# Sums left to accumulating transfers, and transposes taken two blocks at a time: one change to a two-layer trunk on one Trainium2 core

## The chip, the core and the metric

The kernel runs on one NeuronCore of one Trainium2 chip, as one launch. The metric is the device time of the program in microseconds. Before the change it is 2697.47 us, the median of three runs (2697.16 to 2699.16). The engines are called as in the profile: PE is TensorE, DVE is VectorE, ACT is ScalarE, POOL is GpSimd, SP is SyncE, which here only starts transfers; PEld are TensorE's loads of stationary operands.

## What is computed

Two layers over 2048 tokens of 1024 features. Layer 0 is a pooling mixer; it does not change here. Layer 1 projects to queries and a gate z, attends to one shared set of keys and values, multiplies by SiLU(z), projects back, adds the residual, and then adds a gated embedding. Cut to that layer:

```python
def stick_breaking_attention(q, k, v):          # (B, H, S, d), 16 heads of 64
    for blk in range(S // Q_BLOCK):
        logits = q_blk @ k.T * SB_SCALE
        mask = s_idx < t_idx                    # strictly causal
        log_keep = where(mask, log_sigmoid(-logits), 0)
        later = cumsum(log_keep, reverse=True) - log_keep
        a = where(mask, exp(log_sigmoid(logits) + later), 0)
        o = a @ v

x = x + (o * silu(z)) @ b_w_out                 # called x3 in the kernel
x = x + (p[1] @ ple_w[1]) * sigmoid(x @ ple_gate_w[1])
```

All matrices and activations are float32.

## The kernel before

Every activation is held transposed, features on the 128 partitions and tokens along the free axis, in four chunks of 512 tokens (`c` or `s` from 0 to 3). To keep float32 accuracy a matmul is done as three: each operand is split into a rounded half and the rest, both stored as a pair `[P, 2, 512]` (`pr[:, 0]` and `pr[:, 1]`), and high by high, high by low and low by high are summed (L994, L996, L998).

Up to about 1340 us the first layer and all projections run. The attention behind it is one loop over steps `n`. A slot is a query chunk, a head and a key chunk; each has four steps `j`. Query chunks run from 3 down to 0 and have 256, 192, 128 and 64 steps. The stages of one block are set off by numbers of steps:

- `front` (step 4i + j): two matmuls (L924, L925) make the logits of 128 queries by 512 keys in a `psl` buffer; ACT takes their sigmoid into one of four `kap` buffers (L928); `scan` multiplies the remaining stick along the keys on VectorE (L936, on the diagonal L933) into a `pp` tile of the pool `ppool`.
- `turn` (LAG_T = 6 steps behind): for 128 keys `kt`, four transposes on TensorE (L949; on the diagonal 4, 3, 2, 1) turn the `pp` tiles of a slot into a `psa` buffer, of which there are two. ACT copies it rounded into an `at` pair (L952), and VectorE subtracts for the rest (L953); then the buffer is free.
- `gather` (LAG_G = 8 steps behind): two matmuls (L961, L962) of values by the `at` pair add into `pso`. Behind the last one of a head, ACT copies (L976, L977), VectorE adds two halves (L979), ACT adds a bias (L972) and GpSimd multiplies by the gate (L974).

Between these, a generator called `filler` fills TensorE: so many matmuls per step, by the function `shares` for chunks 3 and 2 and by a mean (`even`) for 1 and 0. In chunk 3's stage the filler computes the gates (`gate_z`, with L1028 and L1033); for three of the chunks it takes a `psa` buffer out of turn (L1020), and `load_ends` does so for all four (L910). In the stages of chunks 2, 1 and 0 it is `post(3)`, `post(2)` and `post(1)`; `post(0)` runs alone at the end.

`post(c)` has two halves of eight outputs of 128 features each. In the first, the output projection is added to the residual on VectorE (`xr`, L1068), and `halves` splits the sum into the pair `x3[o]` (ACT L1072, GpSimd L1073). In the second, a gate (`sg`, ACT L1092) is multiplied by the embedding's product `pl` (L1106), and then x3 is added back from its two halves: the low one on GpSimd (L1107), the high one two steps later on VectorE (L1108). `finish` sends the result from SP (L1112), one output later. `xr`, `sg` and others share the tag `tmp` with four buffers.

The order on each engine is set by the program's order for instructions under `keep_in_program_order` (`stay`), and by a scheduler for the others. Every engine works through its own queue in order; SP's transfers wait in that queue too. Around the change stand these lines of the step loop:

```python
for n in range(4 * len(slots) + LAG_G):
    now[0] = n
    i2, j2 = divmod(n - LAG_T, 4)
    if 0 <= i2 < len(slots):
        turn(active[i2], j2)
```

Of the kernel before, what the change touches and what calls it, by code (L numbers as in the profile page):

```python
# [10 lines left out]
F32R = mybir.dt.float32r  # L11
AF = mybir.ActivationFunctionType
ALU = mybir.AluOpType
AX = mybir.AxisListType

P = 128
# [6 lines left out]
W5 = 512  # L23
# [7 lines left out]
def f(ap):  # L31
    return ap.bitcast(F32)
# [3 lines left out]
def trunk_kernel(ctx, tc, x, xt, pt0, wut, cols, heads, zin, grp, aout, agate, aple,  # L36
                 bq, kv, bz, bout, bgate, bple, outt):
    nc = tc.nc
    V, A, G, T = nc.vector, nc.scalar, nc.gpsimd, nc.tensor
# [179 lines left out]
    with ExitStack() as st:  # L219
# [3 lines left out]
        t2 = st.enter_context(tc.tile_pool(name="t2", bufs=2))  # L223
# [631 lines left out]

    with ExitStack() as st:
        kap = st.enter_context(tc.tile_pool(name="kap", bufs=1))
        ppool = st.enter_context(tc.tile_pool(name="ppool", bufs=12))
        t2 = st.enter_context(tc.tile_pool(name="s2", bufs=2))
        psa = st.enter_context(tc.tile_pool(name="psa", bufs=2, space=bass.MemoryType.PSUM))  # L860
        pso = st.enter_context(tc.tile_pool(name="pso", bufs=2, space=bass.MemoryType.PSUM))
# [13 lines left out]
        due, now, tail = [], [0], [0]  # L875

        def soon(k, fn):

            if tail[0]:
                fn()  # L880
                return lambda: None
            item = (now[0] + k, len(due), fn)
            due.append(item)

            def force():
                if item in due:
                    due.remove(item)
                    fn()

            return force  # L890
# [52 lines left out]
        def turn(st, kt):  # L943

            j0 = kt if st["diag"] else 0
            pt = psa.tile([P, W5], F32, tag="psa", name="psa")
            for j in range(j0, 4):
                pp, r0 = st["a"][j]
                T.transpose(pt[:, j * P : (j + 1) * P], pp[:, r0 + kt * P : r0 + (kt + 1) * P], ident)  # L949
            at = t2.tile([P, 2, W5], F32R, tag="at", name="at", bufs=3)  # L950
            cs = slice(j0 * P, W5)
            A.copy(out=at[:, 0, cs], in_=pt[:, cs])  # L952
            V.tensor_tensor(out=at[:, 1, cs], in0=pt[:, cs], in1=f(at[:, 0, cs]), op=ALU.subtract)  # L953
            st["at"][kt] = at
# [89 lines left out]
        def post(c):  # L1044

            pin = t2.tile([P, 2, W5], F32, tag="pin", name="pin", bufs=1)
            nc.sync.dma_start(out=pin, in_=pt0[1, :, c * W5 : (c + 1) * W5].rearrange("(k q) n -> q k n", q=P))
            x3, og, held = [], ogs[c], tc.keep_in_program_order
            while len(og) < 8:
                pair_up(c)  # L1050
            settle()
            both = []
            for o in range(KT):
                xr = t2.tile([P, W5], F32, tag="tmp", name="xr", bufs=4)
                if not c and o < 2:
                    if not o:
                        both = [(stored(wod[e]), dense()) for e in range(2)]
                        for e, (wo, ps) in enumerate(both):
                            yield from piecewise(ps, wo, og, 0, 0, KT - 1)
                    wo, ps = both[o]  # L1060
                    nc.sync.dma_start(out=xr, in_=x2d[c][o])
                    yield from piecewise(ps, wo, og, 0, KT - 1)
                else:
                    wo = stored(wod[o])
                    nc.sync.dma_start(out=xr, in_=x2d[c][o])
                    ps = dense()
                    yield from piecewise(ps, wo, og, 0)
                V.tensor_tensor(out=xr, in0=ps, in1=xr, op=ALU.add)  # L1068
                pr = pair("x3")

                def halves(pr=pr, xr=xr):
                    stay(A.copy(out=pr[:, 0], in_=xr))  # L1072
                    G.tensor_tensor(out=pr[:, 1], in0=xr, in1=f(pr[:, 0]), op=ALU.subtract)  # L1073

                made = soon(1, halves)
                x3.append(pr)
            pt_ = []
            for k in range(2):
                pr = t2.tile([P, 2, W5], F32R, tag="ple", name="ple")
                held(A.copy(out=pr[:, 0], in_=pin[:, k]))  # L1080
                held(V.tensor_tensor(out=pr[:, 1], in0=pin[:, k], in1=f(pr[:, 0]), op=ALU.subtract))
                pt_.append(pr)
            yield
            made()
            late = []
            for o in range(KT):
                wg = stored(wgd[o])
                wl = stored(wld[o])
                ps = dense()
                yield from piecewise(ps, wg, x3, 0)  # L1090
                sg = t2.tile([P, W5], F32, tag="tmp", name="sg", bufs=4)
                made = soon(1, lambda sg=sg, ps=ps: stay(A.activation(out=sg, in_=ps, func=AF.Sigmoid)))  # L1092
                pl = dense()
                yield from piecewise(pl, wl, pt_, 0)
                made()
                if tail[0] and o == KT - 1:
                    whole = t2.tile([P, W5], F32, tag="tmp", name="x3w", bufs=4)
                    V.tensor_tensor(out=whole, in0=f(x3[o][:, 0]), in1=f(x3[o][:, 1]), op=ALU.add)
                    for cs in (slice(0, 256), slice(256, W5)):
                        V.tensor_tensor(out=sg[:, cs], in0=pl[:, cs], in1=sg[:, cs], op=ALU.mult)  # L1100
                        V.tensor_tensor(out=sg[:, cs], in0=sg[:, cs], in1=whole[:, cs], op=ALU.add)
                        if late:
                            late.pop()()
                        nc.sync.dma_start(out=outt[o * P : (o + 1) * P, c * W5 + cs.start : c * W5 + cs.stop], in_=sg[:, cs])
                    continue
                V.tensor_tensor(out=sg, in0=pl, in1=sg, op=ALU.mult)  # L1106
                (V if tail[0] else G).tensor_tensor(out=sg, in0=sg, in1=f(x3[o][:, 1]), op=ALU.add)  # L1107
                summed = soon(2, lambda o=o, sg=sg: V.tensor_tensor(out=sg, in0=sg, in1=f(x3[o][:, 0]), op=ALU.add))  # L1108

                def finish(o=o, sg=sg, summed=summed):  # L1110
                    summed()
                    nc.sync.dma_start(out=outt[o * P : (o + 1) * P, c * W5 : (c + 1) * W5], in_=sg)  # L1112

                if late:
                    late.pop()()
                late.append(finish)
                if c:
                    pair_up(c - 1)
                yield
            if late:  # L1120
                late.pop()()
            yield
# [38 lines left out]
        slots = []  # L1161
# [4 lines left out]
        active, filler, owed, head = {}, beside(NSUB - 1), 0.0, {}  # L1166
        LAG_T, LAG_G = 6, 8
# [19 lines left out]

        for n in range(4 * len(slots) + LAG_G):
            now[0] = n
            i2, j2 = divmod(n - LAG_T, 4)  # L1190
            if 0 <= i2 < len(slots):
                turn(active[i2], j2)
            i, j = divmod(n, 4)
            scan = None
            if i < len(slots):
                c, h, kc = slots[i]
# [91 lines left out]
```

## Time and profile before

| | |
|---|---|
| time, median of three runs | 2697.47 us |
| the profiled execution's own time | 2696.51 us |
| its span, from first to last instruction | 2694.7 us |
| granted TensorE clock over the span | 1.00 |
| transposes L949 | 2176, mean 273 ns |
| L953, rest of the transposed block (VectorE) | 640, mean 596 ns |
| L936, full scan (VectorE) | 384, mean 1336 ns |
| L1107, low half of x3 (GpSimd) | 24, mean 1392 ns |
| L1108, high half of x3 (VectorE) | 31, mean 954 ns |
| VectorE's stand for L1107 before L1108 | 18.1 us in 12 waits |
| transfers' share of the 16 DMA engines, SP's queue | 64.5% |

The mean of a matmul is longer than the distance between two starts, since matmuls are pipelined; starts are what counts. In the rows of a group, the columns are the line, the engine, the operation, the tiles, the number of instructions, then busy time and mean, and the idle time ahead of them with the engine and line that ended it. In a timeline row the first two numbers are the start and the duration, and a bracket holds the idle time ahead of the instruction. A list of waits gives who waited for whom: total, times, and the longest.

### The profile page before, as it was taken

What the parts mean: (1) busy time and instruction counts of PE and PEld (TensorE: products, weight loads), DVE (VectorE), ACT (ScalarE), POOL (GpSimd) and SP (SyncE); (2) the same over time, 40 slices, a digit from 0 to 9 for tenths busy, and PEclk for the clock granted to TensorE, in tenths of its full rate; (3) what the DMA queues carried; (4) which work ended last, traced back from release to release, by engine and by line L of the source; (5) the groups of instructions that cost most, each with busy time, mean ns of one, the idle gap of its engine ahead of it and who ended that gap; (6) DMA issues with size and microseconds to landing.
All of it is one profiled execution on the core that took longest, in us unless ns stands there. A gap on an engine that the chain in (4) does not pass through costs nothing. (4 is left out here: it accounts for less than half of the span.)

```text
span 2694.7 us, 38618 instructions
## 1 busy us (share of the span) xinstructions
PE 2673.6 (99%) x13352; PEld 2226.5 (83%) x13352; DVE 1941.9 (72%) x2506; ACT 1399.0 (52%) x2735; POOL 922.0 (34%) x724
## 2 busy tenths in 40 slices
PE   9999999999999999999999999999999999999999
PEld 8888888888888888888878888888888888888887
DVE  6776626755367643755399999999999998986632
ACT  6445523555135541445366666666666666665531
POOL 2675338643485434753121111122111211222220
PEclk9999999999999999999999999999999999999999
DMA  8657785567856678444788665555655576668865
GB/s 328 222 168 279 252 302 193 198 229 254 300 180 223 242 241 305 145 150 149 223 239 281 195 210 173 163 165 181 198 164 173 173 214 199 197 198 262 268 226 172
DMA packets 276688, 581.56 MB, mean 216 GB/s; under 512 B 33126, under 2 KB 67174, under 8 KB 276492
## 3 DMA queue, kind: packets, MB, share of 16 engines
q1 hardware_dynamic: 270754, 571.41, 64.5%
q10 hardware_dynamic: 5738, 7.68, 1.0%
q8 instruction: 106, 1.74, 0.3%
q14 instruction: 90, 0.74, 0.1%
HBM read 438.40 MB, written 132.19 MB: 212 GB/s over the span
## 5 line engine op out<-in xcount | busy, mean ns | idle before, releaser
L952 ACT CAST at<-psa 128x512 fp32r<-128x512 f32 (+3 forms) x640 | 334.3, 522 | 439.1 <-PE psa L949 429.4
L614 PE MATMUL psd<-wpair,x 128*128 128x512 f32 x2304 | 536.8, 391 | 0.0
L936 DVE TENSOR_TENSOR_SCAN pp<-kap,pp,zeros 128x512 f32<-128x512 f32 x384 | 513.1, 1336 | 6.1 <-ACT kap L928 5.1
L614 PEld LDWEIGHTS psd<-wpair,x 128*128 128x128 f32 x2304 | 429.8, 188 | 87.1
L953 DVE TENSOR_TENSOR at<-psa,at 128x512 fp32r<-128x512 f32 (+3 forms) x640 | 381.3, 596 | 82.0 <-ACT at L952 77.3
L949 PE MATMUL psa<-ident,pp 128*128 128x128 f32 x2176 | 344.6, 273 | 10.7 <-DVE at L953 10.3
L928 ACT ACTIVATE kap<-psl 128x512 f32<-128x512 f32 (+3 forms) x640 | 345.0, 539 | 13.2 <-PE psl L925 10.3
L949 PEld LDWEIGHTS psa<-ident,pp 128*128 128x128 f32 x2176 | 265.4, 140 | 77.7 <-DVE at L953 21.9
L924 PE MATMUL psl<-kk,qa 128*128 128x512 f32 (+3 forms) x640 | 282.3, 441 | 0.1
L962 PE MATMUL pso<-at,vv 128*128 128x512 f32 (+3 forms) x640 | 234.4, 366 | 1.3 <-DVE at L953 1.3
L925 PE MATMUL psl<-kk,qb 128*128 128x512 f32 (+3 forms) x640 | 232.9, 364 | 0.0
L961 PE MATMUL pso<-at,vv 128*128 128x512 f32 (+3 forms) x640 | 232.8, 364 | 0.1
L933 DVE TENSOR_TENSOR_SCAN pp<-kap,ahead 128x128 f32<-128x128 f32 (+3 forms) x256 | 227.0, 887 | 5.1 <-ACT kap L928 3.2
L167 PE MATMUL psd<-xp,wpair 128*128 128x512 f32 x512 | 199.5, 390 | 1.7 <-DVE xp L316 1.7
L166 PE MATMUL psd<-xp,wpair 128*128 128x512 f32 x512 | 200.0, 391 | 0.4 <-ACT xp L315 0.3
L168 PE MATMUL psd<-xp,wpair 128*128 128x512 f32 x512 | 199.3, 390 | 0.0
L149 DVE SCALAR_TENSOR_TENSOR wpair<-wraw,gains,wpair 128x512 fp32r<-128x512 f32 x192 | 161.4, 883 | 48.9 <-ACT wpair L148 48.9
L143 POOL TENSOR_TENSOR wpair<-wraw,wpair 128x512 fp32r<-128x512 f32 x99 | 144.0, 1464 | 84.2 <-ACT wpair L141 78.8
L148 ACT ACTIVATE wpair<-wraw,gains 128x512 fp32r<-128x512 f32 x192 | 132.7, 718 | 68.9 <-DMA wraw<-in_bq_dram 31.1
L1033 POOL TENSOR_TENSOR zr<-zr,sgz 128x512 f32<-128x512 f32 x32 | 62.0, 1938 | 307.1 <-ACT sgz L1032 269.2
L141 ACT CAST wpair<-wraw 128x512 fp32r<-128x512 f32 x148 | 89.9, 618 | 122.1 <-PE psd L168 98.9
L962 PEld LDWEIGHTS pso<-at,vv 128*128 128x128 f32 x640 | 120.3, 188 | 27.7 <-DVE at L953 1.7
(200 smaller groups left out, 5365.7 us busy)
## 6 DMA issues: line engine op xcount, KB each, us to landing
kk<-kd SPq DMA_DIRECT2D x320, 128.0 KB
vv<-vd SPq DMA_DIRECT2D x160, 256.0 KB
wraw<-in_kv_dram SPq DMA_DIRECT2D x128, 256.0 KB
wpair<-wzd SPq DMA_DIRECT2D x64, 512.0 KB
wpair<-wod SPq DMA_DIRECT2D x64, 512.0 KB
wpair<-wgd SPq DMA_DIRECT2D x64, 512.0 KB
wpair<-wu SPq DMA_DIRECT2D x48, 512.0 KB
wpair<-wi SPq DMA_DIRECT2D x36, 512.0 KB
```

Source lines behind the costliest of these rows:

```text
L166: T.matmul(ps, wst(units, kt, 0, c0), acts[kt][:, 0], start=(begin and kt == order[0]), stop=False)
L614: T.matmul(pss2[i], ck["x2"][kt][:, xh, tk], wst(ws, kt, wh, 0, W5), start=(kt == 0 and xh == 0 and wh == 0), stop=(kt == KT - 1 and wh == 1))
L924: T.matmul(ps[:, :w], qa[:, qs], kk[:, :w], start=True, stop=False)
L925: T.matmul(ps[:, :w], qb[:, qs], kk[:, :w], start=False, stop=True)
L928: A.activation(out=kp[:, r0:], in_=ps[:, :w], func=AF.Sigmoid, scale=-1.0)
L933: V.tensor_tensor_scan(out=pp[:, r0:][:, ::-1], data0=kp[:, r0:][:, ::-1], data1=ahead[:, r0:][:, ::-1], initial=1.0, op0=ALU.mult, op1=AL ...
L936: V.tensor_tensor_scan(out=pp[:, ::-1], data0=kp[:, ::-1], data1=zeros.to_broadcast([P, W5]), initial=st["carry"][j], op0=ALU.mult, op1=AL ...
L949: T.transpose(pt[:, j * P : (j + 1) * P], pp[:, r0 + kt * P : r0 + (kt + 1) * P], ident)
L952: A.copy(out=at[:, 0, cs], in_=pt[:, cs])
L953: V.tensor_tensor(out=at[:, 1, cs], in0=pt[:, cs], in1=f(at[:, 0, cs]), op=ALU.subtract)
L961: T.matmul(po[:, cs], vv[:, kt, :], at[:, 0, cs], start=(st["diag"] and kt == 0), stop=False)
L962: T.matmul(po[:, cs], vv[:, kt, :], at[:, 1, cs], start=False, stop=(st["last"] and kt == 3))
```

## The change

There are two parts, and two pools change size with the second.

The first part concerns the query chunks 3 and 2 (`c > 1`). As soon as `xr` is summed, SP writes it to the output (L1072 of the changed kernel). The two adds of x3 are left out; `finish` sends the gated embedding `sg` from GpSimd's queue as a transfer that adds to what lies in the output (L1119). Chunks 1 and 0 stay as they were.

The second part concerns `turn`: in even steps it is called for two blocks, the one that is due and the next, and in odd steps not at all. Every second block is turned one step earlier. `at` has four buffers where it had three, and `ppool` ten where it had twelve.

```diff
-        ppool = st.enter_context(tc.tile_pool(name="ppool", bufs=12))
+        ppool = st.enter_context(tc.tile_pool(name="ppool", bufs=10))
...
-            at = t2.tile([P, 2, W5], F32R, tag="at", name="at", bufs=3)
+            at = t2.tile([P, 2, W5], F32R, tag="at", name="at", bufs=4)
...
                 V.tensor_tensor(out=xr, in0=ps, in1=xr, op=ALU.add)
                 pr = pair("x3")
+
+                if c > 1:
+                    nc.sync.dma_start(out=outt[o * P : (o + 1) * P, c * W5 : (c + 1) * W5], in_=xr)
...
                 V.tensor_tensor(out=sg, in0=pl, in1=sg, op=ALU.mult)
-                (V if tail[0] else G).tensor_tensor(out=sg, in0=sg, in1=f(x3[o][:, 1]), op=ALU.add)
-                summed = soon(2, lambda o=o, sg=sg: V.tensor_tensor(out=sg, in0=sg, in1=f(x3[o][:, 0]), op=ALU.add))
-
-                def finish(o=o, sg=sg, summed=summed):
+                whole = outt[o * P : (o + 1) * P, c * W5 : (c + 1) * W5]
+                summed = lambda: None
+                if c < 2:
+                    (V if tail[0] else G).tensor_tensor(out=sg, in0=sg, in1=f(x3[o][:, 1]), op=ALU.add)
+                    summed = soon(2, lambda o=o, sg=sg: V.tensor_tensor(out=sg, in0=sg, in1=f(x3[o][:, 0]), op=ALU.add))
+
+                def finish(sg=sg, summed=summed, whole=whole):
                     summed()
-                    nc.sync.dma_start(out=outt[o * P : (o + 1) * P, c * W5 : (c + 1) * W5], in_=sg)
+                    if c > 1:
+                        nc.gpsimd.dma_start(out=whole, in_=sg, accum_op=ALU.add)
+                    else:
+                        nc.sync.dma_start(out=whole, in_=sg)
...
             now[0] = n
-            i2, j2 = divmod(n - LAG_T, 4)
-            if 0 <= i2 < len(slots):
-                turn(active[i2], j2)
+            for m in (n, n + 1) if n % 2 == 0 else ():
+                i2, j2 = divmod(m - LAG_T, 4)
+                if 0 <= i2 < len(slots):
+                    turn(active[i2], j2)
```

What this does to the order of the engines is shown at three places, all in the stage of query chunk 2, where the second half of `post(3)` begins.

TensorE, two steps before the change: in each step the transposes, the logits, some matmuls of the filler, and the gather.

```order
L949 MATMUL psa<-ident,pp 128x128 x4
L924 MATMUL psl<-kk,qa 128x512
L925 MATMUL psl<-kk,qb 128x512
L996 MATMUL psd<-og,wpair 128x512
L998 MATMUL psd<-og,wpair 128x512
L961 MATMUL pso<-at,vv 128x512
L962 MATMUL pso<-at,vv 128x512
L949 MATMUL psa<-ident,pp 128x128 x4
L924 MATMUL psl<-kk,qa 128x512
```

The same two steps of the changed kernel:

```order
L949 MATMUL psa<-ident,pp 128x128 x8
L924 MATMUL psl<-kk,qa 128x512
L925 MATMUL psl<-kk,qb 128x512
L996 MATMUL psd<-og,wpair 128x512
L998 MATMUL psd<-og,wpair 128x512
L961 MATMUL pso<-at,vv 128x512
L962 MATMUL pso<-at,vv 128x512
L924 MATMUL psl<-kk,qa 128x512
```

Eight transposes stand where four stood, and the second step begins with its logits. On the diagonal the runs are of seven and three.

VectorE at the first two outputs of that half, before the change (`x_19137` is the pair x3 of the first output; the scan has the operation's name SCALAR_TENSOR_TENSOR here):

```order
L936 SCALAR_TENSOR_TENSOR pp<-kap_12442,pp,zeros 128x512
L1106 TENSOR_TENSOR sg<-psd,sg 128x512
L953 TENSOR_TENSOR at<-psa,at 128x512
L936 SCALAR_TENSOR_TENSOR pp<-kap_12443,pp,zeros 128x512
L1108 TENSOR_TENSOR sg<-sg,x_19137 128x512
L953 TENSOR_TENSOR at<-psa,at 128x512
L936 SCALAR_TENSOR_TENSOR pp<-kap_12444,pp,zeros 128x512
L953 TENSOR_TENSOR at<-psa,at 128x384
L936 SCALAR_TENSOR_TENSOR pp<-kap_12445,pp,zeros 128x512
```

And of the changed kernel, where L1109 is the product that was L1106:

```order
L953 TENSOR_TENSOR at<-psa,at 128x512 x2
L936 SCALAR_TENSOR_TENSOR pp<-kap_12442,pp,zeros 128x512
L1109 TENSOR_TENSOR sg<-psd,sg 128x512
L936 SCALAR_TENSOR_TENSOR pp<-kap_12443,pp,zeros 128x512
L953 TENSOR_TENSOR at<-psa,at 128x512
L953 TENSOR_TENSOR at<-psa,at 128x384
L936 SCALAR_TENSOR_TENSOR pp<-kap_12444,pp,zeros 128x512
L936 SCALAR_TENSOR_TENSOR pp<-kap_12445,pp,zeros 128x512
```

The L953 stand in twos ahead of two scans, and the add L1108 is gone.

SP's queue of the changed kernel around the first of the new writes (`wod`, the weights of the output projection; `qd`, `kd`, `vd`, the stored queries, keys and values):

```order
L212 DMA wpair<-wod_275 128x1024
L1072 DMA out_dram<-xr 128x512
L192 DMA qa<-qd_2_210 64x512 x2
L193 DMA qb<-qd_2_210 64x512 x2
L1065 DMA xr<-x2d_4_132 128x512
L212 DMA wpair<-wod_276 128x1024
L200 DMA kk<-kd_2_242 64x512 x2
```

The row L1072 is new; the loads behind it wait with it.

## The prediction, as it was put on record

> **What bounds the kernel now.** I read the page's busy table first, then the same table by stage of the attention, then the list of waits, and last the timeline around single waits.
>
> ```profile
> span 2694.7 us, 38618 instructions
> PE 2673.6 (99%) x13352; PEld 2226.5 (83%) x13352; DVE 1941.9 (72%) x2506; ACT 1399.0 (52%) x2735; POOL 922.0 (34%) x724
> ```
>
> TensorE is busy for 99% of the span. The change removes no matmul, so it can win only what TensorE idles (21 us in all) or a cost between its instructions. It touches the attention alone, which I cut into stages by query chunk (three rows: chunk 3, chunk 2, chunk 1; columns: length, busy time of PE, PEld, DVE, ACT, POOL, clock, DMA share, GB/s):
>
> ```profile
> 1361.00:1889.00 528.00, 524.34 (x2897) 436.81 (x2898) 514.06 (x614) 342.77 (x687) 89.82 (x49) 1.00 0.65 201
> 1889.00:2200.00 311.00, 306.91 (x1704) 256.83 (x1703) 302.25 (x370) 203.60 (x422) 53.70 (x32) 1.00 0.57 180
> 2200.00:2440.00 240.00, 236.76 (x1310) 199.42 (x1309) 213.04 (x278) 153.04 (x336) 46.12 (x31) 1.00 0.69 204
> ```
>
> VectorE is nearly as full as TensorE in chunks 3 and 2 (514 of 528 and 302 of 311 us). Who keeps TensorE waiting stands in the list of waits, taken for the same three stretches (the first from 1340) and for the end of the attention:
>
> ```profile
> PE psa L949 <- DVE at L953: 3.0, 6, 1.2
> PE psae L910 <- DVE at L953: 0.6, 1, 0.6
> ...
> PE psa L949 <- DVE at L953: 4.1, 5, 1.0
> ...
> PE psa L949 <- DVE at L953: 3.2, 6, 1.1
> ...
> PE pso L962 <- DVE at L953: 1.3, 1, 1.3
> ```
>
> It is always one wait: the transposes (L949) write a psa buffer that VectorE (L953) has not emptied yet. There are 3.0, 4.1 and 3.2 us of it in chunks 3, 2 and 1. How one arises, in chunk 1:
>
> ```profile
> 2333.47 1.29 POOL L1107 TENSOR_TENSOR sg<-sg,x 128x512 f32<-128x512 f32 x1 [13.12 <-PE psl L925]
> ...
> 2334.79 1.76 DVE L1108 TENSOR_TENSOR sg<-sg,x 128x512 f32<-128x512 f32 x1 [0.99 <-POOL sg L1107]
> ...
> 2336.47 1.27 DVE L936 TENSOR_TENSOR_SCAN pp<-kap,pp,zeros 128x512 f32<-128x512 f32 x1
> ...
> 2336.68 0.34 PE L962 MATMUL pso<-at,vv 128*128 128x384 f32 x1
> 2337.67 0.39 DVE L953 TENSOR_TENSOR at<-psa,at 128x256 fp32r<-128x256 f32 x1
> ...
> 2338.11 0.66 PE L949 MATMUL psa<-ident,pp 128*128 128x128 f32 x4 [1.10 <-DVE at L953]
> ```
>
> VectorE stands 0.99 us for GpSimd's add, adds for 1.76, then owes a scan and the L953 that TensorE needs. TensorE idles 1.10.
>
> **First part of the change: the sums of chunks 3 and 2 leave VectorE and GpSimd.** In chunk 2 (first row) and chunk 1 (second row) the final add costs VectorE
>
> ```profile
> L1108 DVE TENSOR_TENSOR sg<-sg,x 128x512 f32<-128x512 f32 x8 | 9.6, 1195 | 0.8 <-POOL sg L1107 0.8
> ...
> L1108 DVE TENSOR_TENSOR sg<-sg,x 128x512 f32<-128x512 f32 x7 | 9.0, 1284 | 5.6 <-POOL sg L1107 5.6
> ```
>
> so 9.6 + 0.8 us in chunk 2 and 9.0 + 5.6 in chunk 1 disappear from it (the eighth of the second set falls just behind 2440). That alone is worth nothing; it counts where a TensorE wait follows. Four of the five waits of chunk 2 and five of the six of chunk 1 start within 3.5 us behind an L1108. The first and the last of these nine pairs, and the one wait of chunk 1 that is no pair:
>
> ```profile
> 2063.09 1.70 DVE L1108 TENSOR_TENSOR sg<-sg,x 128x512 f32<-128x512 f32 x1
> ...
> 2065.45 0.55 PE L949 MATMUL psa<-ident,pp 128*128 128x128 f32 x3 [0.30 <-DVE at L953]
> ...
> 2407.43 1.77 DVE L1108 TENSOR_TENSOR sg<-sg,x 128x512 f32<-128x512 f32 x1 [1.12 <-POOL sg L1107]
> ...
> 2409.85 0.66 PE L949 MATMUL psa<-ident,pp 128*128 128x128 f32 x4 [0.63 <-DVE at L953]
> ...
> 2439.24 0.63 PE L949 MATMUL psa<-ident,pp 128*128 128x128 f32 x4 [0.27 <-DVE at L953]
> ```
>
> Each of the nine is shorter (at most 1.10) than the VectorE time that goes ahead of it (the add with its stand), so I let all nine go. They hold 4.1 - 1.04 = 3.0 us of idle time in chunk 2 and 3.2 - 0.27 = 3.0 in chunk 1. The one that stays in chunk 2 (1.04) has another cause, a GpSimd product beside a scan:
>
> ```profile
> 2050.63 1.27 DVE L936 TENSOR_TENSOR_SCAN pp<-kap,pp,zeros 128x512 f32<-128x512 f32 x1
> ...
> 2052.21 1.29 POOL L974 TENSOR_TENSOR os<-os,zt 128x512 f32<-128x512 f32 x1 [10.67 <-ACT os L972]
> 2052.41 2.17 DVE L936 TENSOR_TENSOR_SCAN pp<-kap,pp,zeros 128x512 f32<-128x512 f32 x1
> ...
> 2053.78 0.40 PE L962 MATMUL pso<-at,vv 128*128 128x512 f32 x1
> ...
> 2055.22 0.66 PE L949 MATMUL psa<-ident,pp 128*128 128x128 f32 x4 [1.04 <-DVE at L953]
> ```
>
> Beside GpSimd's product the scan takes 2.17 us instead of 1.27, so removing sixteen GpSimd adds also spares scans; I count that inside the nine waits. The same rows show what a wait costs: L949 starts 1.44 us after L962 where 0.23 is the rule, so 1.21 are lost where the view says 1.04. With 0.17 more for each of nine, the term is **-(3.0 + 3.0 + 1.5) = -7.5 us**; its bounds are 0 (VectorE owes the time elsewhere) and -9.2 (all eleven waits of chunks 2 and 1).
>
> What replaces the adds: sixteen more 256 KB writes on SP's queue (L1072) and sixteen accumulating transfers of 256 KB on GpSimd's queue in the place of L1107. The trace has no accumulating transfer. GpSimd is busy 54 of 311 and 46 of 240 us; if issuing one cost it as much as the add's 1.3 us, nothing on TensorE's path would notice, and if it cost nothing, neither. But if it slowed scans as the add does, part of the 7.5 would stay: between 0 and +4, and I take 0, since the row nearest to it is a transfer, not an add that reads two tiles. SP waits in order, and behind L1072, which waits for L1068, stand loads of qa, kk and vv. The waits of SP between 1889 and 2440:
>
> ```profile
> SPq L1112 <- DVE sg L1108: 32.1, 11, 5.1
> ...
> SPq L1065 <- POOL x L1073: 24.4, 8, 6.2
> ```
>
> SP already stood up to 5.1 us for L1108 in the same way, and 6.2 for an xr buffer, without any TensorE wait on a transfer in the list above. L1112 leaves SP for these chunks while L1072 comes: 0, with 0 to +3 as bounds. The transfers hold sg longer, but tmp has four buffers, so an sg comes back four outputs later, and chunk 2's stage makes sixteen outputs in 311 us, 19 us each: 78 us later, no wait.
>
> **Second part: two blocks' transposes together.** Is there a cost at the joint between transposes and matmuls? One transpose between full matmuls, then four:
>
> ```profile
> 1704.93 0.39 PE L962 MATMUL pso<-at,vv 128*128 128x512 f32 x1
> ...
> 1705.16 0.27 PE L949 MATMUL psa<-ident,pp 128*128 128x128 f32 x1
> ...
> 1705.50 0.39 PE L925 MATMUL psl<-kk,qb 128*128 128x512 f32 x1
> ...
> 1460.87 0.39 PE L962 MATMUL pso<-at,vv 128*128 128x512 f32 x1
> 1461.10 0.60 PE L949 MATMUL psa<-ident,pp 128*128 128x128 f32 x4
> ...
> 1461.77 0.39 PE L925 MATMUL psl<-kk,qb 128*128 128x512 f32 x1
> ```
>
> From L962 to L925 are 0.57 us with one and 0.90 with four: 0.11 for each transpose. Two full matmuls take 0.46, so 0.57 - 0.46 - 0.11 leaves nothing for the joint, within 0.01. 320 joints go: between -3 and +3 us, and I take **-1**, since the same difference over all undisturbed groups (31 with one, 189 with four) is 0.000 to 0.007.
>
> The Trainium skill ("TensorE: Matmul & The Clock Gate", Part 2, step 1) has a rule against this: weight loads are pulled ahead of running matmuls. By it the first load of each group hides behind L962, a merged pair hides one load instead of two, and with the page's 128/1.2 = 107 ns against 56 ns for the matmul 320 x 0.05 = 16 us are lost. The rows do not agree: one transpose costs the same 0.11 as each of four, since L924 behind it is late in turn (0.48 us long where L925 has 0.39).
>
> The price is the double buffer. Before, VectorE alternates L953 and scan; now it does two L953, then two scans. A pair's second group needs the second L953, which ends 0.68 behind the first (row below), while the first group gives 4 x 0.11 = 0.44: the margin shrinks by 0.25 at each pair. How often is it that thin? A transpose's weight load may start with the matmul ahead, 0.23 early, so its waits in chunk 3 count the thin places:
>
> ```profile
> PEld psa L949 <- DVE at L953: 9.1, 17, 1.6
> ...
> L953 DVE TENSOR_TENSOR at<-psa,at 128x512 fp32r<-128x512 f32 x123 | 83.0, 675 | 5.8 <-ACT at L952 4.5
> ```
>
> 17 of 256 steps. Those in the middle of a pair vanish as places, so I take ten: 10 x 0.25 = **+2.5**, bounds 0 and 128 pairs x 0.25 = +32. Of the 3.0 us in chunk 3 a part stands at odd steps, whose check goes, but most of that lateness reappears at the next pair: **-1**, a third, with -3 and 0 as bounds. Seven places take a psa buffer out of turn (L910, L1020); behind a pair that buffer was filled in the same step, but three matmuls now stand ahead of it: **+0.5**, bounds 0 and 7 x 0.6 = +4. The last block is turned one step earlier, which shortens the wait of 1.3 at the end: **-0.5**, bounds -1.3 and 0. ScalarE (343 of 528 us) and the smaller ppool (next use two steps behind the last reading) cost nothing.
>
> **Sum:** -7.5 - 1 + 2.5 - 1 + 0.5 - 0.5 = -7.0 us. The profiled execution took 2696.5 us (span 2694.7), 1.0 below the median of the three runs, 2697.5. Against the median the forecast is **2690.5 us**.
>
> **The rivals.** *The waits only move* (0.10): VectorE's bursts in chunks 2 and 1 also come from L1068, L979 and L1106, and pairs are checked more strictly, so half of the 7.5 is given back: 2694. For it speaks the wait at 2055, which has no L1108; against it that nine of eleven have one. *The transfers disturb as the adds did* (0.10): issuing them slows scans, or SP's loads come late: +4, 2694.5, or with SP's +3 about 2697. *Pairs starve TensorE* (0.12, the slower side): in chunk 3, where nothing is relieved and VectorE has 14 us of air in 528, the second group of a pair waits its 0.25 routinely. Ten pairs are in the sum; beyond the seven won and 5.4 more it needs 12.4/0.25, so 50 further pairs: from 60 of 128 on the kernel is slower, and with all it stands at 2720. For it speaks VectorE's 97%; against it that only 17 steps are thin now. *A merged pair loses half a transpose* (0.02), 0.055 at each of 320 pairs, since only one weight load of a run stands free: 17.6 us, 2709; the two groups measured above speak against it. (That is the Trainium skill's rule of the pull-ahead.) *Better than forecast* (0.06): all waits of chunks 3 to 1 go and pairs cost nothing: 2678 to 2684. That the scheduler undoes the pairs is excluded: the order of TensorE shows runs of seven and eight.
>
> **How the numbers follow.** The forecast has 0.60 with its own range of 2684 to 2695. A measurement can tell about 0.2% (5.4 us) from no change, so the lines are 2692.1 and 2702.9. Of the 0.60, 0.50 lie below; with 0.06, faster has 0.56. Same has 0.10 of the forecast and both middle rivals, 0.30. Slower has 0.14. The range 2682 to 2701 leaves out about 0.04 below and 0.14 above.
>
> **What would show it.** Right: waits of L949 for L953 in chunks 2 and 1 fall from 7.3 us to about 1.5, chunk 3 has 3 to 6, eight transposes take 0.88 us from first start to the next matmul, and no wait on a transfer appears. Wrong: chunk 3's waits above 12 us (pairs starve), scans of 2 us beside the GpSimd transfers, or TensorE waits named after kk, vv or wod.

## The result, and the profile after

The changed kernel takes **2689.52 us** (median of eight runs, 2688.59 to 2690.98) beside 2697.22 us for the kernel before on the same chip (eight runs, 2695.92 to 2699.16). The ratio is 0.9971, with a 95% interval of 0.9962 to 0.9981: 7.7 us faster. Two executions in the experiments, one of the kernel before (6391 us, beside runs 8 and 10 to 12) and one of run 11 (3630 us), were far slower than all others and are in no median below. The forecast was 2690.5 us, range 2682 to 2701. Lines of the changed kernel have new numbers: L1109 is the product that was L1106, L1072 the new write, L1119 the accumulating transfer.

The head of the page of the changed kernel, and its group of transposes (instructions, busy time and mean, idle time ahead of them):

```profile
span 2688.0 us, 39378 instructions
...
PE 2673.2 (99%) x13352; PEld 2237.9 (83%) x13352; DVE 1917.1 (71%) x2490; ACT 1391.2 (52%) x2735; POOL 904.0 (34%) x724
...
L949 PE MATMUL psa<-ident,pp 128*128 128x128 f32 x2176 | 295.6, 274 | 4.4 <-DVE at L953 3.9
```

TensorE does the same work (2673.2 us where it was 2673.6), and the span is 6.7 us shorter: nearly all that went is idle time. The same three stretches as in the prediction, and in them the waits of TensorE (the first two rows belong to 1340 to 1889, the third to 1889 to 2200; from 2200 to 2592 there is none):

```profile
1361.00:1889.00 528.00, 522.87 (x2882) 439.31 (x2881) 511.71 (x611) 338.86 (x683) 82.66 (x47) 1.00 0.64 200
1889.00:2200.00 311.00, 310.41 (x1729) 264.29 (x1727) 295.23 (x367) 205.21 (x428) 49.57 (x33) 1.00 0.63 191
2200.00:2440.00 240.00, 239.97 (x1335) 204.97 (x1333) 208.63 (x275) 152.57 (x339) 42.70 (x32) 1.00 0.75 218
```

```profile
PE psa L949 <- DVE at L953: 3.4, 6, 1.4
PE psae L910 <- DVE at L953: 1.1, 1, 1.1
...
PE psa L949 <- DVE at L953: 0.6, 1, 0.6
```

In the second and third stretch TensorE is busy for 310.4 of 311 and 240.0 of 240 us; the 4.1 and 3.2 us of waits are 0.6 and 0. The first stretch has 4.5 us where it had 3.6, and the wait at the end of the attention is gone.

These stretches are the stages of the filler. The logits of a query chunk begin 26 to 80 us ahead of these bounds, so the work of a chunk is better cut at its first logits. In the timeline these are the starts for chunk 3, 2, 1 and 0 and, fifth, the last L962 of the attention, of the kernel before and then of the changed one:

```profile
1332.78 0.22 PE L924 MATMUL psl<-kk,qa 128*128 128x128 f32 x1
...
1809.04 0.30 PE L924 MATMUL psl<-kk,qa 128*128 128x128 f32 x1
...
2164.59 0.30 PE L924 MATMUL psl<-kk,qa 128*128 128x128 f32 x1
...
2414.29 0.31 PE L924 MATMUL psl<-kk,qa 128*128 128x128 f32 x1
...
2591.75 0.33 PE L962 MATMUL pso<-at,vv 128*128 128x128 f32 x1 [1.28 <-DVE at L953]
```

```profile
1333.44 0.22 PE L924 MATMUL psl<-kk,qa 128*128 128x128 f32 x1
...
1812.07 0.30 PE L924 MATMUL psl<-kk,qa 128*128 128x128 f32 x1
...
2165.48 0.31 PE L924 MATMUL psl<-kk,qa 128*128 128x128 f32 x1
...
2409.53 0.30 PE L924 MATMUL psl<-kk,qa 128*128 128x128 f32 x1
...
2584.07 0.28 PE L962 MATMUL pso<-at,vv 128*128 128x128 f32 x1
```

By differences, chunk 3 takes 476.3 us before and 478.6 after, chunk 2 355.5 and 353.4, chunk 1 249.7 and 244.1, and chunk 0 to the last L962 177.5 and 174.5. So the change loses 2.4 us in chunk 3 and wins 2.1, 5.7 and 2.9 behind it; 0.7 of the last is given back between the last L962 and the last matmul (98.3 and 99.0 us).

### The profile page after: what moved, and what is told of

It is laid out like the page before. It is cut to its first block, busy times and chain, and to the rows that moved or that the text cites. A ratio compares the mean times of both kernels' runs of the same rounds, so it can differ in the third digit from the quotient of the medians.

```text
span 2688.0 us, 39378 instructions
## 1 busy us (share of the span) xinstructions
PE 2673.2 (99%) x13352; PEld 2237.9 (83%) x13352; DVE 1917.1 (71%) x2490; ACT 1391.2 (52%) x2735; POOL 904.0 (34%) x724
## 3 DMA queue, kind: packets, MB, share of 16 engines
HBM read 438.40 MB, written 136.38 MB: 214 GB/s over the span
## 4 chain that ended last, share of the span: by engine, by line
PE 94%; DVE 3%; DMA 1%; issue 1%; ACT 0%; SPq 0%; DVEq 0%; ACTq 0%
PE psd L614 19%; PE psd L166 9%; PE psd L167 9%; PE psd L168 9%; PE psa L949 8%; PE psd L994 6%; PE psd L998 6%; PE psd L996 6%; PE psl L925 4%; PE pso L962 4%; PE pso L961 4%; PE psl L924 4%; DVE pp L936 2%; PE pst L719 1%; PE psdt L994 1%
## 5 line engine op out<-in xcount | busy, mean ns | idle before, releaser
L936 DVE TENSOR_TENSOR_SCAN pp<-kap,pp,zeros 128x512 f32<-128x512 f32 x384 | 507.1, 1339 | 11.2 <-ACT kap L928 7.2
L952 ACT CAST at<-psa 128x512 fp32r<-128x512 f32 (+3 forms) x640 | 304.2, 525 | 221.1 <-PE psa L949 218.8
L953 DVE TENSOR_TENSOR at<-psa,at 128x512 fp32r<-128x512 f32 (+3 forms) x640 | 357.2, 599 | 58.5 <-ACT at L952 55.6
L949 PE MATMUL psa<-ident,pp 128*128 128x128 f32 x2176 | 295.6, 274 | 4.4 <-DVE at L953 3.9
L949 PEld LDWEIGHTS psa<-ident,pp 128*128 128x128 f32 x2176 | 250.6, 141 | 42.3 <-DVE at L953 14.3
L924 PE MATMUL psl<-kk,qa 128*128 128x512 f32 (+3 forms) x640 | 256.3, 401 | 0.1
L933 DVE TENSOR_TENSOR_SCAN pp<-kap,ahead 128x128 f32<-128x128 f32 (+3 forms) x256 | 215.0, 853 | 42.6 <-ACT kap L928 40.7
L925 PE MATMUL psl<-kk,qb 128*128 128x512 f32 (+3 forms) x640 | 233.8, 365 | 0.0
L962 PE MATMUL pso<-at,vv 128*128 128x512 f32 (+3 forms) x640 | 233.4, 365 | 0.0
L1033 POOL TENSOR_TENSOR zr<-zr,sgz 128x512 f32<-128x512 f32 x32 | 55.4, 1732 | 314.6 <-ACT sgz L1032 235.4
L962 PEld LDWEIGHTS pso<-at,vv 128*128 128x128 f32 x640 | 120.2, 188 | 25.3
```

The costliest lines, as they stand in the source:

```text
L924: T.matmul(ps[:, :w], qa[:, qs], kk[:, :w], start=True, stop=False)
L925: T.matmul(ps[:, :w], qb[:, qs], kk[:, :w], start=False, stop=True)
L936: V.tensor_tensor_scan(out=pp[:, ::-1], data0=kp[:, ::-1], data1=zeros.to_broadcast([P, W5]), initial=st["carry"][j], op0=ALU.mult, op1=AL ...
L962: T.matmul(po[:, cs], vv[:, kt, :], at[:, 1, cs], start=False, stop=(st["last"] and kt == 3))
```

## The experiments

All twelve runs in one table. The last five columns are worked out for each kernel from its trace as above, in us: the lengths of the chunks 3, 2 and 1, then from the first logits of chunk 0 to the last L962, and from there to the end of the last matmul. The kernel before took 2697.75 us beside runs 1 to 4, 2696.89 beside 5 to 7 and 9, and 2697.00 beside 8 and 10 to 12, which are from another chip than the rest. The ratios are not the quotients of these medians, from which they differ by up to 0.0005. Differences below some 2 us between two kernels are within these intervals.

| run | time, us | ratio, 95% | chunk 3 | chunk 2 | chunk 1 | chunk 0 | tail |
|---|---|---|---|---|---|---|---|
| before | 2697.22 | 1 | 476.3 | 355.5 | 249.7 | 177.5 | 98.3 |
| after | 2689.52 | 0.9971 (0.9962-0.9981) | 478.6 | 353.4 | 244.1 | 174.5 | 99.0 |
| 1 transfers alone | 2689.68 | 0.9971 (0.9960-0.9981) | 476.7 | 352.2 | 245.0 | 177.5 | 98.3 |
| 2 pairs alone | 2699.81 | 1.0008 (0.9999-1.0017) | 478.4 | 356.5 | 251.6 | 174.5 | 98.9 |
| 3 pairs from chunk 2 on | 2687.53 | 0.9967 (0.9954-0.9979) | 476.3 | 354.0 | 244.0 | 174.5 | 99.0 |
| 4 no sum at all | 2688.71 | 0.9969 (0.9957-0.9980) | 478.3 | 353.4 | 244.0 | 174.6 | 98.9 |
| 5 transfers and pools | 2689.47 | 0.9975 (0.9965-0.9984) | 476.0 | 352.2 | 245.0 | 177.5 | 98.3 |
| 6 pairs from chunk 1 on | 2686.97 | 0.9964 (0.9950-0.9978) | 476.1 | 352.2 | 245.4 | 174.5 | 99.0 |
| 7 both adds on VectorE | 2690.23 | 0.9975 (0.9966-0.9984) | 476.3 | 351.8 | 246.0 | 178.4 | 98.4 |
| 8 GpSimd's add only | 2688.46 | 0.9964 (0.9949-0.9979) | 475.9 | 351.3 | 244.1 | 178.0 | 100.0 |
| 9 second group later | 2688.04 | 0.9969 (0.9958-0.9980) | 477.1 | 352.2 | 245.2 | 174.6 | 99.0 |
| 10 VectorE's add later | 2690.68 | 0.9974 (0.9963-0.9985) | 475.9 | 352.5 | 245.3 | 178.2 | 98.3 |
| 11 adds on VectorE, late pairs | 2689.49 | 0.9969 (0.9956-0.9982) | 475.9 | 351.8 | 248.4 | 174.6 | 99.0 |
| 12 VectorE's add only | 2687.76 | 0.9962 (0.9949-0.9976) | 476.0 | 351.3 | 244.4 | 177.4 | 98.4 |

### 1 and 2: each part alone

Run 1 has the write L1072, the accumulating transfer and no adds for `c > 1`, with the pools and `turn` of before. Run 2 has only this:

```diff
-            i2, j2 = divmod(n - LAG_T, 4)
-            if 0 <= i2 < len(slots):
-                turn(active[i2], j2)
+            for m in (n, n + 1) if n % 2 == 0 else ():
+                i2, j2 = divmod(m - LAG_T, 4)
+                if 0 <= i2 < len(slots):
+                    turn(active[i2], j2)
```

with four `at` buffers and ten in `ppool`.

> The first part alone: chunks 3 and 2 by accumulating transfers, transposes one block per step, pools as before. Mine (the gain is TensorE's waits behind L1108, so it comes with the transfers): 2689.5 to 2691, so at least 6 us of the change's 7.7; the waits of L949 for L953 between 1889 and 2440 fall from 7.3 us to under 2.5, those from 1340 to 1889 stay at 3.0. Rival (the pairs won it, since half of the checks on psa are gone): 2695 to 2697, with waits of 5 us or more left between 1889 and 2440.

> The second part alone: transposes in pairs, with its pools, sums on GpSimd and VectorE as before. Mine: between 2696 and 2699, no gain, since the 2.4 us that the stretch of chunk 3's fronts lost in the changed kernel stand against 2.5 us less at the end of the attention; the waits between 1889 and 2440 stay at 5 to 9 us. Rival (pairs won it): 2689 to 2692. If the two parts need each other (neither alone gives 4 us): both e1 and e2 between 2693 and 2697.

TensorE's waits of run 1 (1340 to 1889; 1889 to 2200; 2200 to 2440; the end), then those of run 2 in the same stretches (at the end it has none):

```profile
PE psa L949 <- DVE at L953: 3.0, 6, 1.2
...
PE psa L949 <- DVE at L953: 0.6, 3, 0.2
...
PE psa L949 <- DVE at L953: 0.3, 1, 0.3
...
PE pso L962 <- DVE at L953: 1.3, 1, 1.3
```

```profile
PE psa L949 <- DVE at L953: 3.4, 6, 1.4
PE psae L910 <- DVE at L953: 1.1, 1, 1.1
...
PE psa L949 <- DVE at L953: 3.5, 5, 1.3
...
PE psa L949 <- DVE at L953: 4.0, 5, 1.3
```

The transfers alone have the whole gain: 2689.68 beside 2689.52. Pairs alone are no gain, and rather a loss: 2699.81 is 0.8 above the range expected for them. The two lists answer each other: run 1 loses the waits of chunks 2 and 1 and keeps that of the end; run 2 loses the one at the end and keeps the others. Run 1 has one wait more, of 0.2 us for a load of kk, but at 1402 us, long before the first of the new transfers.

### 3, 6 and 9: where pairs cost

Runs 3 and 6 are the changed kernel with pairs only from chunk 2 or from chunk 1 on (256 and 448):

```diff
-            for m in (n, n + 1) if n % 2 == 0 else ():
+            for m in ((n, n + 1) if n % 2 == 0 else ()) if n - LAG_T >= 448 else (n,):
```

Run 9 is the changed kernel with the second of the two `turn` calls put behind `front`, so that the logits stand between the two groups.

> The changed kernel with pairs only for the blocks of query chunks 2, 1 and 0; chunk 3 turns one block per step. Mine (pairs cost where VectorE is not relieved): 2686.5 to 2688.5, faster than the changed kernel by 1 to 3 us, and the first 256 fronts last 476 us again instead of 478.6. Rival (the 2.4 us are scatter, or come from the pools of ten and four): 2689 to 2691, fronts at 478 us or more.

> The changed kernel with pairs only for the blocks of query chunks 1 and 0. In e1 (no pairs) the four front stretches and the end took 476.7, 352.2, 245.0, 161.4 and 16.1 us, in the changed kernel 478.6, 353.4, 244.1, 160.9 and 13.6. Mine (pairs cost where VectorE is full, and pay where it has air): 476.5, 352.2, 244.1, 160.9, 13.6, hence 2686 to 2688. Rival (no gain left beyond e3): 2688.5 or more.

> The changed kernel, but in even steps the second block's transposes stand behind the logits of the step (L924, L925) instead of directly behind the first block's. VectorE's order then alternates again: L953, scan, L953, scan. Mine (what a pair costs is the thinner margin of its second group on the psa buffer: that group now needs an L953 that stands behind one more scan, so its margin is some 0.7 us thinner than the pair's): the first 256 fronts take 480 us or more, time 2692 to 2700. Rival (what costs is the bunching on ScalarE and VectorE, which alternation undoes): fronts at 476 to 477 us, time 2686 to 2689.

Without pairs in chunk 3 that chunk takes 476.3 and 476.1 us again: the 2.4 us lost there are the pairs' doing. Run 3 still has 354.0 in chunk 2 where run 1 has 352.2, so pairs cost there too; run 6 has 352.2, and keeps the 2.9 us won in chunk 0. In chunk 1 it takes 245.4 where 244.1 had been expected: pairs won nothing there. At 2686.97 us it has the lowest time of all kernels that compute everything, 2.7 us below run 1 and 2.5 below the changed kernel, though their intervals overlap. In run 9 chunk 3 takes 477.1 us, against an expected loss, and the time is where the rival had put it: waits of the second group grew (by distances of starts, from 2.2 to some 4 us in chunk 3), but those of the first, which now stands a scan further from the L953 ahead of it, fell (3.9 to 1.5). That expectation took the two groups as if they stood alone.

### 4 and 5: what the transfers and the pools cost

Run 4 is the changed kernel with no write of `xr` and a plain write from SP in place of the accumulating transfer. Run 5 is run 1 with the pools of the changed kernel; TensorE and VectorE have the same order as in run 1.

> Leaves out a part of the computation: in chunks 3 and 2 the output is the gated embedding alone, x3 is not added; no write of xr and no accumulating transfer, sg leaves from SP's queue. All else as in the changed kernel. It measures what the transfers cost. Mine (their price is 0): within 1.5 us of the changed kernel, 2688 to 2691. Rival (issuing them slows scans, or SP's loads come late): 2684 to 2687.5, 2 to 5 us faster than the changed kernel.

> The first part alone, as e1, but with the pools of the second part: ppool 10 and at 4 instead of 12 and 3. It tells whether the 2.1 us that pairs cost chunk 3's fronts come from the pools. Mine (pools cost nothing): 2688.5 to 2691, the first 256 fronts at 476 to 477 us. Rival (the smaller ppool holds the scans): fronts at 478 us or more, time 2691 to 2694.

Without the sum 2688.71, with it 2689.52, and the chunks are equal to 0.3 us. The intervals do not tell the 0.8 us from nothing; run 4 still writes sg, so what it prices is the sixteen additional writes and the accumulating. The pools cost nothing (2689.47 beside 2689.68).

### 7, 8, 10 and 12: which part of the adds made the waits

Four versions of the kernel before, without transfers and pairs. Run 7 has both adds on VectorE in chunks 3 and 2:

```diff
-                (V if tail[0] else G).tensor_tensor(out=sg, in0=sg, in1=f(x3[o][:, 1]), op=ALU.add)
+                (V if tail[0] or c > 1 else G).tensor_tensor(out=sg, in0=sg, in1=f(x3[o][:, 1]), op=ALU.add)
```

Run 8 keeps L1107 and drops L1108 there, run 12 drops L1107 and keeps the other, and run 10 only moves it back:

```diff
-                summed = soon(2, lambda o=o, sg=sg: V.tensor_tensor(out=sg, in0=sg, in1=f(x3[o][:, 0]), op=ALU.add))
+                summed = soon(4, lambda o=o, sg=sg: stay(V.tensor_tensor(out=sg, in0=sg, in1=f(x3[o][:, 0]), op=ALU.add)))
```

> The kernel before with one edit: in chunks 3 and 2 the add of the low half (L1107) also runs on VectorE; no transfers, no pairs. VectorE then adds twice per output, but never stands for GpSimd and no add shares its time. If VectorE's own time for the add is what counts: 2697 to 2700, no gain, waits between 1889 and 2440 at 6 to 9 us. If the stand for GpSimd and the adds lengthened beside it (1.70 instead of 0.66) are what counts: 2691 to 2694, waits of 2 to 4 us. I hold the second likelier, at about half of the gain.

> The kernel before, with GpSimd's add (L1107) as it was in chunks 3 and 2 and VectorE's add (L1108) left out there, so the high half of x3 is missing from those outputs; no transfers of the change, no pairs. It parts the two adds. If VectorE's owed add and its stand make the waits (the recorded reason), nothing of them is left without L1108: 2689 to 2691, waits of L949 for L953 under 2 us in chunks 2 and 1 together. If a GpSimd add beside a scan is enough to make them, as the wait at 2055 suggests: 2694 or more, with most of the 7.3 us of waits still there.

> The kernel before, with GpSimd's add (L1107) left out in chunks 3 and 2 and VectorE's add (L1108) kept, so the low half of x3 is missing from those outputs. VectorE does as many instructions as before, but stands for nobody and no GpSimd add lies beside its scans. If the amount of VectorE's work makes the waits: 2694 or more. If the burst made with GpSimd makes them, as the run with both adds on VectorE suggests: 2688.5 to 2690.5, waits of L949 for L953 under 2 us in chunks 2 and 1, and L1108 near 0.7 us each in place of 1.2.

> The kernel before with L1108 two steps later (about three scans), pinned there; GpSimd's add stays where it is, and nothing is left out. VectorE no longer stands for L1107. If the stand and the meeting with GpSimd's next product make the waits: 2690 to 2693, the stand before L1108 falls from 6.4 us to under 1, L1108 to 0.7 to 0.9 us each. If VectorE's added work or GpSimd's add beside a scan makes them: 2695 or more.

Each of the four is enough. In chunks 2 and 1 together the kernel before takes 605.3 us, and these take 597.9 (run 7), 595.4 (run 8), 595.7 (run 12) and 597.9 (run 10). Groups of VectorE between 1889 and 2440 us, first the two adds of run 7, then the one of run 12, then that of run 10:

```profile
L1107 DVE TENSOR_TENSOR sg<-sg,x 128x512 f32<-128x512 f32 x16 | 13.6, 850 | 0.1
...
L1108 DVE TENSOR_TENSOR sg<-sg,x 128x512 f32<-128x512 f32 x16 | 12.8, 798 | 0.1
```

```profile
L1109 DVE TENSOR_TENSOR sg<-sg,x 128x512 f32<-128x512 f32 x16 | 14.6, 913 | 0.1
```

```profile
L1108 DVE TENSOR_TENSOR sg<-sg,x 128x512 f32<-128x512 f32 x16 | 12.8, 798 | 0.8 <-POOL sg L1107 0.8
```

In run 7 VectorE spends 26.4 us on the adds, more than the 18.5 and 6.4 of stand that the kernel before has in this stretch (fifteen adds), and the waits are gone all the same. So it is not the amount of VectorE's work. In run 8 GpSimd adds as before, and the scans beside it are as long as before (L936 1337 ns on the mean, 1321 before), so it is not GpSimd's add either. It is the meeting of the two in one place: either add alone is harmless, and so are both when the second comes later. A long add alone is not enough: in run 12 four of the sixteen still take 1.52 to 1.72 us behind another GpSimd operation (hence the mean of 913 ns where about 0.7 us had been expected), and no wait follows. Run 10 holds the opposite case: its last add of chunk 2's stage still comes soon behind L1107, stands 0.81 us for L1107 and takes 1.76, and the wait behind it (2193, 0.96 us) is there as before. For run 7 half of the waits had been expected to stay, since VectorE would owe the same time; that theory fell here. Here is one of the waits of the kernel before, from GpSimd's add to the late transposes (timeline: start, duration):

```profile
2103.23 1.30 POOL L1107 TENSOR_TENSOR sg<-sg,x 128x512 f32<-128x512 f32 x1 [3.62 <-PE pso L962]
...
2103.62 1.99 DVE L933 TENSOR_TENSOR_SCAN pp<-kap,ahead 128x512 f32<-128x512 f32 x1
...
2104.50 2.22 POOL L1007 TENSOR_TENSOR og<-os,og 128x512 fp32r<-128x512 f32 x1
...
2105.54 1.72 DVE L1108 TENSOR_TENSOR sg<-sg,x 128x512 f32<-128x512 f32 x1
...
2107.19 0.68 DVE L953 TENSOR_TENSOR at<-psa,at 128x512 fp32r<-128x512 f32 x1
...
2107.92 0.66 PE L949 MATMUL psa<-ident,pp 128*128 128x128 f32 x4 [0.89 <-DVE at L953]
```

The ends tell it: L1107 ends at 2104.53, the scan 1.08 later (2105.61), GpSimd's next operation, the split L1007, 1.11 later (2106.72), the add L1108 0.54 later (2107.26). None of the four gets on while the one ahead of it, on the other engine, is running; the two engines take turns. L953, which TensorE needs, stands behind the chain. The same place in run 10, where L1107 and L1007 are unchanged and only L1108 is gone from between:

```profile
2103.49 1.30 POOL L1107 TENSOR_TENSOR sg<-sg,x 128x512 f32<-128x512 f32 x1 [3.62 <-PE pso L962]
...
2103.88 1.99 DVE L933 TENSOR_TENSOR_SCAN pp<-kap,ahead 128x512 f32<-128x512 f32 x1
...
2104.75 2.22 POOL L1007 TENSOR_TENSOR og<-os,og 128x512 fp32r<-128x512 f32 x1
...
2105.79 0.66 DVE L953 TENSOR_TENSOR at<-psa,at 128x512 fp32r<-128x512 f32 x1
...
2107.13 0.60 PE L949 MATMUL psa<-ident,pp 128*128 128x128 f32 x4
```

L953 runs at its 0.66 us beside L1007, is done 2.96 us behind the start of L1107 (4.64 in the kernel before), and TensorE does not wait. L953 reads PSUM and one tile of SBUF, L1108 two tiles of SBUF, and only the second kind takes turns with GpSimd. Of the fifteen adds L1108 that the kernel before has between 1889 and 2440 us, eight are stretched to 1.70 us or more in this way, and seven of the nine waits named in the prediction come behind one of these; the other two come behind an add of 0.69 us that had stood for L1107.

### 11: adds on VectorE and late pairs

> Both adds of x3 on VectorE in chunks 3 and 2, no transfers of the change, and pairs only from chunk 1 on. Pairs from chunk 1 on saved 2.7 us beside the transfers (2686.97 against 2689.68). If the two savings are independent: 2686.5 to 2688.5. If pairs take back what the adds on VectorE leave thin: 2689.5 or more.

It is run 7 with the pairs of run 6. The end is won (174.6) but chunk 1 takes 248.4 us in place of 246.0; the two longest losses at transposes there, by distances of starts, stand at the second group of a pair (0.9 and 0.8 us). With the adds still on VectorE, pairs take back what they give.

## Why the prediction was right, by its steps

The sum was right (7.7 us against 7.0). Most terms hold one by one; some of those that concern pairs were wrong in size, and that they cancel (forecast +0.5 together, measured about 0) is luck.

**The waits behind L1108, -7.5.** Chunks 2 and 1 are shorter by 8.1 us in run 1 and by 7.8 in the changed kernel. The four runs above show the reason given for them: a VectorE that stands for GpSimd's add, adds slowly, and then owes the L953. One sentence of that step was too wide: that sixteen GpSimd adds fewer also spare scans counted inside the nine waits. In run 8 the scans are not spared and the waits go. And the step let the wait of 1.04 at 2055 stay, since it has no L1108 within reach; it is gone as well, and one of 0.6 at 2026 is new. That wait hangs on who comes first: the long scan starts 0.20 us behind GpSimd's product L974 in the kernel before, and 0.18 behind it in run 10, where the wait stays (1.03). In runs 7, 8 and 12 VectorE is a little earlier, the scan starts 0.26 to 0.86 us ahead of the product and takes its 1.27, the product waits instead, and TensorE does not.

**The transfers, 0.** For the changed kernel this holds as far as run 4 can tell, and no TensorE wait names a transfer there. But in run 1 the rival that issuing them slows scans is seen on a small scale. Four scans between 2121 and 2189 us that begin 0.21 to 0.22 us behind such an issue, with a GpSimd operation right behind the issue, take 2.54 to 3.08 us. The last of them, and TensorE behind it:

```profile
2188.13 0.88 POOL L1119 DMA_DIRECT2D out_dram<-sg  x1 [3.85 <-DVE sg L1109]
2188.35 3.08 DVE L936 TENSOR_TENSOR_SCAN pp<-kap,pp,zeros 128x512 f32<-128x512 f32 x1
2188.75 1.59 POOL L1007 TENSOR_TENSOR og<-os,og 128x512 fp32r<-128x512 f32 x1
...
2191.93 0.33 PE L949 MATMUL psa<-ident,pp 128*128 128x128 f32 x1 [0.20 <-DVE at L953]
```

The scan ends 1.09 behind L1007, though it began 0.40 ahead of it. By distances of starts TensorE loses 1.4 us at the transposes behind these four; three of them are the waits of 0.6 in run 1's list. Runs 8 and 12, without such transfers, do not lose it, and are shorter than run 1 by 1.8 and 1.5 us in chunks 2 and 1, most of it there. So two errors offset in run 1: without the adds' waits 9.5 to 9.9 us go (runs 12 and 8; the step's bound was 9.2), and the transfers take about 1.4 back. Why the scan loses its turn is open, and it is a close race: in these four the GpSimd operation starts 0.39 to 0.40 us behind the scan, while at 2060 and 2101 in the same kernel it starts 0.41 behind and the scan keeps its turn.

**The joints, -1.** Seven transposes of the changed kernel between full matmuls:

```profile
2250.74 0.39 PE L962 MATMUL pso<-at,vv 128*128 128x512 f32 x1
2250.97 0.93 PE L949 MATMUL psa<-ident,pp 128*128 128x128 f32 x7
2251.65 0.48 PE L924 MATMUL psl<-kk,qa 128*128 128x512 f32 x1
2251.96 0.40 PE L925 MATMUL psl<-kk,qb 128*128 128x512 f32 x1
```

From L962 to L925 are 1.22 us; less 0.46 for two full matmuls, that is 0.109 for each of seven. Over all undisturbed groups eight take 0.875 us beyond the 0.46 where two groups of four take 0.879: 0.004 for each of 320 pairs, 1.3 us. (From their first start to the next matmul eight take 0.79; the 0.88 expected is counted to L925.) The rival that a merged pair loses half a transpose is out, and with it the rule of the Trainium skill ("TensorE: Matmul & The Clock Gate", Part 2) as it was applied to these transposes: what the first of a group gains, L924 behind the last one loses (0.48 us long in the row above, where L925 has 0.40).

**The second group of a pair, +2.5 in chunk 3.** The mechanism is there. The first pair at which it shows:

```profile
1359.76 1.26 DVE L953 TENSOR_TENSOR at<-psa,at 128x512 fp32r<-128x512 f32 x2
1359.88 0.40 PE L962 MATMUL pso<-at,vv 128*128 128x512 f32 x1
...
1360.47 1.25 PE L949 MATMUL psa<-ident,pp 128*128 128x128 f32 x8 [0.20 <-DVE at L953]
...
1361.48 0.48 PE L924 MATMUL psl<-kk,qa 128*128 128x512 f32 x1
```

TensorE waits 0.20 for the first L953, and from there to L924 are 1.01 us, where undisturbed eights have 0.79. By the starts of the single transposes, 0.06 of the 0.22 is lost at the second, behind the first group's wait, and 0.11 and 0.06 at the fifth and sixth, in the second group. Twelve places in chunk 3 lose 0.16 or more in this way (ten were taken, at 0.25) and two about 0.1, 2.2 us in all. The step took the two L953 as ending 0.68 apart; two that stand together end 0.6 apart (x2 take 1.26, one 0.66), and 0.6 - 0.44 is the 0.16 found. So the size came out by a higher count and a lower price.

**The odd steps, -1,** did not come: by distances of starts the first groups of chunk 3 lose 3.9 us after, 4.0 before. **The buffers out of turn, +0.5,** were 0.8 (L910 0.6 to 1.1, and 0.3 at L1020). With the second groups this makes 2.2 - 0.1 + 0.8 = 2.9 us; less the 128 joints at 0.004, 0.5, it is the 2.4 lost in chunk 3.

**Left out:** pairs in chunk 2. The step priced them in chunk 3 alone, since VectorE is relieved in the others; between run 1 and the changed kernel chunk 2 loses 1.2 us.

**The end of the attention, -0.5,** was mis-sized the other way: 2.9 us between the first logits of chunk 0 and the last L962, with 0.7 back in the tail. The step counted a part of the wait of 1.3 alone; of the other 1.6, 0.3 is the wait at 2439, which the prediction let stay; what the rest consists of was not tried.

In sum, pairs cost 3.2 us in chunks 3 and 2 and win about as much behind them (run 1 to the changed kernel, by the columns of the table: +2.0, +1.2, -1.0, -2.9, +0.7), so the whole gain is the first part's. Of the rivals, "the waits only move" fell with run 1, "the transfers disturb" with run 4, but for the 1.4 us seen in run 1; "pairs starve TensorE" is real in kind (run 2 is 0.08% above the kernel before, within its interval) but far from the point at which it decides: fourteen thin second groups in chunk 3, not sixty.

What stays open: why the four scans of run 1 lose their turn, and whether the 2.5 us between run 6 and the changed kernel are all there, for their intervals overlap (by the columns of one execution each it is 2.4). Pairs in chunk 0 alone, and run 8's or run 12's order in a kernel that computes everything, were not tried.

## What to carry to other kernels

An add that waits for another engine's add is dear by its place, not by its length: before removing work from a full engine, try it two steps later, or both halves on one engine, which here had 6 to 7 of the 7.7 us without the transfers. Where two engines take turns, look for a chain of their instructions whose last link stands ahead of the one that the bounding engine needs, and move that link. Grouping work under a double buffer lost here where the buffer's owner was full and won at the end, so give it to such stages alone.

## What the runs showed of the hardware

- VectorE instructions with two tiles of SBUF and GpSimd's sums, differences and products take turns. In the kernel before, between 1889 and 2440 us, all eight stretched adds L1108 (1.70 to 1.77 us, alone 0.66) end 0.55 us behind the end of a GpSimd operation, and all twenty full scans L936 of 1.33 us or more (1.33 to 2.32, alone 1.27) end 1.08 or 1.09 behind one, whatever their own length. None of the L953 is over 0.69 us there, beside GpSimd or not. The Trainium skill ("SBUF — State Buffer", section "SBUF: two separate sides") has this as an exclusive lock between VectorE with two SBUF inputs and GpSimd; the trace agrees, within 0.01 us in these 28 instructions. In the four scans of run 1 above, the one that began first did not go first: they began ahead of the GpSimd operation and ended behind it.
- An accumulating transfer of 256 KB is cheaper to issue than the add it replaces. The row of L1119 in the changed kernel (duration on GpSimd in ns, minimum, median and maximum), and its time to landing:

```profile
L1119 POOL DMA_DIRECT2D out_dram<-sg x16: 862/875/1094, 2045.4 to 2434.1; - x16
...
DMA to landing us min/median/max: 4.1/5.3/7.8
```

It takes GpSimd 0.88 us where the add took 1.41. In the changed kernel it lengthens no full scan: four beside an issue take 1.66 us, and each ends 1.08 or 1.09 behind a GpSimd operation that began before it. In run 1 four are long beside one, as shown above. The bytes that the page counts as read from HBM do not rise with it:

```profile
HBM read 438.40 MB, written 136.38 MB: 214 GB/s over the span
```

438.40 was read before too, and 132.19 written; the 4.19 more are the sixteen new writes.
